# Output gates of heads 0 to 6 computed ahead of the mixers, six of them by seven products, and the scans moved under the next head's q and k

## The chip, the cores and the metric

One core of a Trainium2 chip runs the whole block. The metric is device microseconds from start to end of the program. The kernel before takes 1549.74 us (median of three runs, 1549.45 to 1550.22).

## What is computed

The block takes 1024 frames of 1024 features, sets 16 learned meta tokens ahead of them (T = 1040 tokens), and mixes tokens by eight heads of two kinds: four mLSTM heads with input and forget gates, four retention heads with rotary positions. The parts that matter here, in the reference's terms:

```python
u = rmsnorm(x, mix_g)
# per head: q, k (128 wide), v (256 wide), output gate o (256 wide), all u @ w_in
h = mlstm_chunkwise(conv_silu(q), conv_silu(k), v, li, lf)     # heads 0 to 3
h = retention_chunkwise(rotary(q), rotary(k), v, log_gamma)    # heads 4 to 7
mixed = head_norm(h, g) * (sigmoid(o) if mLSTM else silu(o))
x = x + mixed @ w_out
x = x + gated_conv_mlp(rmsnorm(x, ffn_g))
```

The output gate o of a head needs nothing but u and its weights; it is used only where the scan's normalized output is mixed.

## The kernel before

Every product in float32 accuracy is made of three TensorE passes: both operands are split into a high and a low part (hi on ACT, lo = x - hi on DVE), and hi*hi, hi*lo, lo*hi are summed in PSUM. u is held as such pairs, uh and ul, eight blocks of 128 features by 1040 tokens.

**The mixers.** A first phase makes v of head 0 chunk by chunk as the input lands, with the first norm beside it (`first_norm`, `rms`: row sums by TensorE, square root on ACT, reciprocal on DVE, broadcast back by TensorE into tiles named pra). Then come q and k of head 0, with `gates` (the mLSTM gates: scans along rows on DVE, two rows stored to DRAM as `scr`) and `tables` (which reads them back into the tables A1 and A2, broadcast to all partitions). Then each head h goes through three stages:

- o: `o_group`, six groups (two halves of 128 gate columns by three pieces of 386, 384 and 256 tokens). Under them run the head's first scans: `scan_a` (scores, masks, splits) and `scan_b` (numerator, state), chunks 0 to 3.
- v of head h+1: `v_group`, nine chunks. Under them the rest of the scans and `post_steps` of head h: head norm, transposes (tiles tr), the mixing with the gate (tile mx), and its store to DRAM (`mxd`).
- q and k of head h+1: `qk_group`, six groups with convolution or rotation on DVE. Nothing runs under these.

`merge` deals the side work out among the main groups in code order; a list scheduler then sets each engine's own order, so that all that is said on positions below is read from the finished order.

**Weights.** `units` is a list of weight blocks in the order of their use; `need` asks for one and issues some blocks ahead. A raw block (512 KB) goes into one of two slots (`raw_tile`), its hi and lo parts into one of three. A raw slot is free again when hi and lo have been made of it. Two blocks of w_out per head ("m" units, `last_two`) are used otherwise: they stay in their slot until DVE has multiplied them with the mixed values of the last two tokens (tile mm) and added them to acc, twice 128x1024. In the list they stand after the o blocks of the next head, ahead of v: o(h), o(h), m(h-1), m(h-1), v(h+1), v(h+1), q(h+1), k(h+1).

**Behind the mixers** come w_out, up and gate, and down, each by seven block products in place of eight (Strassen's scheme): sums of weight blocks and of activation blocks are made once, and tiles of 256 and 258 columns are multiplied. The weight sums are made by DMA (`wsum`), dealt out over the mixers' stages.

Of the kernel before, what the change touches and what calls it, by code (L numbers as in the profile page):

```python
# [31 lines left out]
XW = SEQ // 2 + 2  # L32
EPS = 1e-6
# [28 lines left out]
def body(ctx, tc, h_in, vecs, cst, mask_in, rot, w_v0, w_v, w_fm, w_out, w_up, w_gate, w_down, out):  # L62
# [3 lines left out]
    per = ctx.enter_context(tc.tile_pool(name="per", bufs=1))  # L66
    wraw = ctx.enter_context(tc.tile_pool(name="wraw", bufs=2))
# [14 lines left out]
    resid = per.tile([P, KB, T], F32, name="resid")  # L82
# [3 lines left out]
    accseg = ExitStack()  # L86
    accp = accseg.enter_context(tc.tile_pool(name="accp", bufs=1, side="right"))

    acc = accp.tile([P, 2, D], F32, name="acc")
    mm = accp.tile([P, 2 * 8, 2], F32, name="mm")  # L90
    rring = []
    mixed = ExitStack()
    mxp = mixed.enter_context(tc.tile_pool(name="mxp", bufs=1, side="right"))
    mxd = [dram.tile([P, SEQ], F32, name=f"mxd{i}") for i in range(16)]
    epsc = per.tile([P, 1], F32, name="epsc")
    Rb = per.tile([P, T], F32, name="Rb")

# [13 lines left out]


# [20 lines left out]
    def issue(upto):  # L133
        while issued[0] < min(upto, len(units)):
# [8 lines left out]
            sub = 2 if key[:2] == ("v", 0) else 1  # L143
# [61 lines left out]

    u_v(0)
# [108 lines left out]
    mix = ExitStack()  # L315
    st = mix.enter_context(tc.tile_pool(name="st", bufs=1))
    wk = mix.enter_context(tc.tile_pool(name="wk", bufs=2))

    cols = st.tile([P, 3, R36], F32, name="cols")
    dec = st.tile([P, R36], F32, name="dec")  # L320
    sigs = [st.tile([P, 2, PIECES[1][1] - KEEP], F32, name="sig"), mxp.tile([P, 2, T - PIECES[2][0]], F32, name="sig2")]

    def sig(b, p):
        t0, t1, _ = PIECES[p]
        return sigs[1][:, b] if p == 2 else sigs[0][:, b, max(t0, KEEP) - KEEP:t1 - KEEP]
    gts = st.tile([P, 2, NCH, H], F32, name="gts")
    nc.gpsimd.memset(gts[:, :, 0, :], 0.0)
    scr = dram.tile([2, R36, P], F32, name="scr")

    Rc = st.tile([P, NCH], F32, name="Rc")  # L330
    Rg = st.tile([P, H, NCH], F32, name="Rg")
    ug = st.tile([P, KB, 32], F32, name="ug")
    mask = st.tile([P, P], F32, name="mask")
# [56 lines left out]
    def qk_group(h, kind, p):  # L390
# [7 lines left out]
        if h < H:  # L398
# [13 lines left out]
            if h == 0 and kind == "q" and p == 0:  # L412
                after(x, last["sqrt"])
# [102 lines left out]
    def tables(h):  # L516
        if h > H:
            return
# [476 lines left out]
    for h in range(8):  # L995
# [4 lines left out]
        if h == 7:  # L1000
            break
# [6 lines left out]

# [576 lines left out]
```

## Time and profile before

| | |
|---|---|
| median of three runs | 1549.74 us |
| the profiled execution | 1551.16 us, span 1549.4 us |
| granted TensorE clock, mean | 0.992 |
| start of q of head 0, end of the first phase | 37.6 us |
| start of the o gates of head 0 | 64.0 us |
| o gates, v, q and k of one head, heads 4 and 5 | 28.22, 31.23, 23.96 us |
| start of w_out | 701.7 us |

A row of a profile names the source line, the engine, the operation, what is written and read, the count, and after the bar the busy time and the mean of one in ns, then the idle time of the engine ahead of it and what ended it. In rows of windows, each engine's busy time in that stretch follows its length; then come the granted clock, the DMA share and GB/s.

### The profile page before, as it was taken

The numbers are of one execution on the slowest core, as the hardware profiler recorded it, in microseconds if no ns is written. First come the engines' busy times: TensorE is split into PE (matmuls) and PEld (weight loads), VectorE is DVE, ScalarE is ACT, GpSimd is POOL, SyncE is SP. The second block draws the span as 40 slices with busy tenths as digits, with TensorE's granted clock in tenths as the row PEclk, the third lists the DMA queues.
The fourth block names the chain that finished last, engine by engine and source line by source line (L and its number), as shares of the span: only waits on it lengthen the run. The fifth ranks groups of instructions, "written<-read, shape, count | busy, mean of one in ns | idle before, by whom it ended". The sixth has DMA issues, their size and how long they took to land.

```text
span 1549.4 us, 25346 instructions
## 1 busy us (share of the span) xinstructions
PE 1520.5 (98%) x9763; PEld 1398.9 (90%) x9763; DVE 1085.4 (70%) x2312; ACT 735.2 (47%) x1491; POOL 90.5 (6%) x107
## 2 busy tenths in 40 slices
PE   8989999999999999999999999999999999999997
PEld 8989999999999999997788998999999999888887
DVE  8756758686866565678867778766666666778657
ACT  7565555554242433435454455444444444434443
POOL 0110112112120210000000000000000000000000
PEclk9999999999999999999999999999999999999998
DMA  5676768778777773226542225332222224933213
GB/s 190 153 165 165 137 160 193 167 189 181 192 167 179 148 160 90 64 74 245 189 138 97 87 95 185 102 102 83 82 82 82 76 82 142 378 103 111 95 41 109
DMA packets 104904, 212.35 MB, mean 137 GB/s; under 512 B 9352, under 2 KB 31568, under 8 KB 104784
## 3 DMA queue, kind: packets, MB, share of 16 engines
q1 hardware_dynamic: 86096, 175.80, 33.9%
q0 software_dynamic: 18544, 34.87, 14.9%
q8 instruction: 76, 1.25, 0.3%
q14 instruction: 44, 0.36, 0.1%
q10 hardware_dynamic: 144, 0.07, 0.0%
HBM read 181.31 MB, written 84.19 MB: 171 GB/s over the span
## 4 chain that ended last, share of the span: by engine, by line
PE 93%; DMA 3%; DVE 2%; ACT 1%; SPq 0%; issue 0%; DVEq 0%; ACTq 0%
PE pv L374 4%; PE po L386 4%; PE po L384 4%; PE po L385 4%; PE pv L375 4%; PE pv L376 4%; PE pdx L554 3%; PE pdx L556 3%; PE pdx L555 3%; PE pup_x L555 2%; PE pup_x L556 2%; PE pga_x L554 2%; PE pga_x L556 2%; PE pga_x L555 2%; PE pup_x L554 2%; PE pk L384 2%
## 5 line engine op out<-in xcount | busy, mean ns | idle before, releaser
L374 PE MATMUL pv<-hi_v,uh 128*128 128x256 f32 (+1 forms) x512 | 148.4, 290 | 7.6 <-DVE sig L428 3.6
L375 PE MATMUL pv<-lo_v,uh 128*128 128x256 f32 (+1 forms) x512 | 147.6, 289 | 0.0
L376 PE MATMUL pv<-hi_v,ul 128*128 128x256 f32 (+1 forms) x512 | 145.8, 286 | 0.0
L384 PE MATMUL po<-uh,hi_o 128*128 128x386 f32 (+2 forms) x384 | 124.7, 325 | 0.0
L386 PE MATMUL po<-uh,lo_o 128*128 128x386 f32 (+2 forms) x384 | 122.6, 319 | 0.0
L385 PE MATMUL po<-ul,hi_o 128*128 128x386 f32 (+2 forms) x384 | 122.5, 319 | 0.0
L374 PEld LDWEIGHTS pv<-hi_v,uh 128*128 128x128 f32 x512 | 98.2, 192 | 11.6 <-DVE sig L428 3.8
L375 PEld LDWEIGHTS pv<-lo_v,uh 128*128 128x128 f32 x512 | 98.1, 192 | 0.8 <-DVE lo_v L150 0.8
L376 PEld LDWEIGHTS pv<-hi_v,ul 128*128 128x128 f32 x512 | 97.9, 192 | 0.0
L243 ACT CAST hi_up<-raw_up 128x512 fp32r<-128x512 f32 (+1 forms) x52 | 36.4, 719 | 106.7 <-PE pga_z L555 61.2
L384 PEld LDWEIGHTS po<-uh,hi_o 128*128 128x128 f32 x384 | 72.4, 188 | 0.2
L385 PEld LDWEIGHTS po<-ul,hi_o 128*128 128x128 f32 x384 | 72.4, 188 | 0.1
L386 PEld LDWEIGHTS po<-uh,lo_o 128*128 128x128 f32 x384 | 72.3, 188 | 0.0
L244 DVE TENSOR_TENSOR lo_ga<-fraw_ga,hi_ga 128x512 fp32r<-128x512 f32 (+1 forms) x52 | 41.8, 807 | 37.8 <-ACT hi_ga L243 37.6
L554 PE MATMUL pup_x<-uh_g,hi_up 128*128 128x256 f32 (+1 forms) x240 | 67.2, 282 | 0.4 <-ACT uh_g L1024 0.4
L555 PE MATMUL pup_x<-ul_g,hi_up 128*128 128x256 f32 (+1 forms) x240 | 67.4, 283 | 0.1
L244 DVE TENSOR_TENSOR lo_up<-raw_up,hi_up 128x512 fp32r<-128x512 f32 (+1 forms) x52 | 41.3, 808 | 36.0 <-ACT hi_up L243 35.2
L556 PE MATMUL pup_x<-uh_g,lo_up 128*128 128x256 f32 (+1 forms) x240 | 66.3, 282 | 0.0
L194 POOL DMA_DIRECT2D wsd<-w_down_d x55 | 50.9, 1026 | 262.8 <-DMA wsd<-w_down_d 166.1
L384 PE MATMUL pq<-uh,hi_q 128*128 128x400 f32 (+2 forms) x192 | 62.2, 324 | 3.7 <-DVE vl L350 2.5
L385 PE MATMUL pq<-ul,hi_q 128*128 128x400 f32 (+2 forms) x192 | 62.4, 325 | 0.0
L386 PE MATMUL pk<-uh,lo_k 128*128 128x400 f32 (+2 forms) x192 | 62.1, 324 | 0.0
(751 smaller groups left out, 5009.9 us busy)
## 6 DMA issues: line engine op xcount, KB each, us to landing
wsd<-w_down_d SPq DMA_DIRECT2D x22, 512.0 KB, 6.6
wsd<-w_down_d POOLq DMA_DIRECT2D x22, 512.0 KB, 6.5
raw_up<-w_up_d SPq DMA_DIRECT2D x22, 512.0 KB, 3.9
fraw_ga<-w_gate_d SPq DMA_DIRECT2D x22, 512.0 KB, 3.9
acts<-cv SPq DMA_DIRECT2D x44, 256.0 KB, 2.0
rd<-wsd SPq DMA_DIRECT2D x22, 512.0 KB, 3.3
wsd<-w_down_d POOLq DMA_DIRECT2D x33, 256.0 KB, 5.1
raw_o<-w_fm_d SPq DMA_DIRECT2D x16, 512.0 KB, 3.8
```

The source lines that it names most:

```text
L194: nc.gpsimd.dma_start(x, v, accum_op=ALU.add)
L243: nc.scalar.copy(hi[:, o:o + n], x)
L244: nc.vector.tensor_tensor(lo[:, o:o + n], x, hi[:, o:o + n].bitcast(F32), ALU.subtract)
L374: nc.tensor.matmul(pv[:L, :nv], a, hi[:, o:o + nv], start=kb == 0, stop=False)
L375: nc.tensor.matmul(pv[:L, :nv], a, lo[:, o:o + nv], start=False, stop=False)
L376: nc.tensor.matmul(pv[:L, :nv], b, hi[:, o:o + nv], start=False, stop=kb == KB - 1)
L384: nc.tensor.matmul(pt[:, :n], a, uh[kb][:, t0:t1], start=kb == 0, stop=False)
L385: nc.tensor.matmul(pt[:, :n], a, ul[kb][:, t0:t1], start=False, stop=False)
L386: nc.tensor.matmul(pt[:, :n], b, uh[kb][:, t0:t1], start=False, stop=kb == KB - 1)
L554: m.append(nc.tensor.matmul(pt, ah, xh_, start=first and k == 0, stop=False, skip_group_check=True))
L555: nc.tensor.matmul(pt, ah, xl_, start=False, stop=False, skip_group_check=True)
L556: m.append(nc.tensor.matmul(pt, al, xh_, start=False, stop=last and k == n - 1, skip_group_check=True))
```

## The change

- Gates of head 0 are made in the first phase, as the input lands (`o_first`), in place of v of head 0; their product with the norm goes to DRAM (`sgd`) by way of two tiles.
- `ocomb` then builds four combinations of the halves of u (tokens and features each in two halves) from the residual tile, in place, and splits them in hi and lo.
- `o_seven` makes the gates of heads 1 to 6, by seven products each over blocks of 256 and 258 columns, and stores them to `sgd`. `ostep` makes the weight sums on DVE. `sgload` reads a head's gates back when it is mixed.
- v of head 0 is now a stage of its own, with nothing under it; then q and k of head 0.
- Head h below 7: the first scans run under q and k of head h+1, the rest and `post_steps` under v of head h+1. The o stage is gone, except for head 7, which keeps the old form. Tables A and the q and k tiles are there twice, in the place of the residual, which is read again from the input at head 7.
- The mixed values are written over the gate tile (`sig`), no longer into mx.
- The list of weights is: o0, o1 to o6 (four steps each), v0, q0, k0, then q(h+1), k(h+1), m(h-1), m(h-1), v(h+1), v(h+1).

```diff
+    u_f(0, "o")
+    ou = [(h, s) for h in range(1, 7) for s in range(4)]
+    ou.insert(ou.index((1, 1)), ou.pop(ou.index((2, 0))))
+    for h, s in ou:
+        units.append((("o", h, s), lambda h=h, s=s: ostep(h, s)))
     u_v(0)
     u_f(0, "q")
     u_f(0, "k")
-    for h in range(8):
-        u_f(h, "o")
+    for h in range(7):
+        u_f(h + 1, "q")
+        u_f(h + 1, "k")
         if h:
             u_m(h - 1)
-        if h < 7:
-            u_v(h + 1)
-            u_f(h + 1, "q")
-            u_f(h + 1, "k")
+        u_v(h + 1)
+    u_f(7, "o")
+    u_m(6)
...
+    def ocomb():
...
+        for k in range(4):
+            nc.scalar.activation(B4[k], B4[k], AF.Copy, scale=g4[k])
+            nc.vector.scalar_tensor_tensor(B4[k], B1[k], g1[k], B4[k], ALU.mult, ALU.subtract)
+            nc.vector.tensor_tensor(B1[k], B1[k], A1_[k], ALU.subtract)
+            nc.vector.scalar_tensor_tensor(A1_[k], A1_[k], g1[k], B4[k], ALU.mult, ALU.subtract)
...
+            put(4, k, A1_[k])
+        for k in range(4):
+            put(3, k, B1[k], g1[k])
+        for k in range(4):
+            put(5, k, B4[k])
+        for k in range(4):
+            nc.vector.scalar_tensor_tensor(A4[k], A4[k], g4[k], A1_[k], ALU.mult, ALU.subtract)
+            put(6, k, A4[k])
...
+    def o_seven(h):
...
+        for n, (bank, s, o, x) in enumerate(PROD):
+            hi, lo = need(("o", h, s), 2)
+            xs = oblk(x)
+            for ci, (j0, j1) in enumerate(OC):
...
+                m = mm3s(pt, [tuple(v[:, o * HB + k * P:o * HB + (k + 1) * P] for v in (hi, lo)) for k in range(4)],
+                         [tuple(v[:, j0:j1] for v in xs[k]) for k in range(4)], n in (0, 1, 3), n in (1, 5, 6))
...
-        merge([lambda b=b, p=p: (o_group(h, b, p), p == 1 and wsum_next()) for b in range(2) for p in range(3)],
-              [A(0)] + [B(c) for c in range(4 if h < 7 else NCH)])
         if h == 7:
+            resid = rp.tile([P, KB, T], F32, name="resid2", tag="R")
+            for kb in range(0, KB, 2):
+                nc.sync.dma_start(resid[:, kb:kb + 2], h_in[:, kb:kb + 2])
+        for p in range(3):
+            sgload(h, p)
+        if h == 7:
+            merge([lambda b=b, p=p: o_group(h, b, p) for b in range(2) for p in range(3)], [A(0)] + [B(c) for c in range(NCH)])
             break
+        tables(h + 1)
+        merge([lambda kind=kind, p=p: (qk_group(h + 1, kind, p), (kind, p) == ("k", 0) and wsum_next()) for kind in "qk" for p in range(3)], [A(0)] + [B(c) for c in range(4)])
         side = post_steps(h, 0) + [B(4), B(5), B(6)] + post_steps(h, 1) + [B(7), B(8)] + post_steps(h, 2)
         merge([lambda c=c: (v_group(h + 1, c)(), c == 4 and wsum_next()) for c in range(NCH)], side)
-        tables(h + 1)
-        for kind in "qk":
-            for p in range(3):
-                qk_group(h + 1, kind, p)
```

**How the instructions move.** First DVE, around the second accumulation of head 4's last tokens (acc from raw_m9). Before, it stands among the evacuations of k of head 5 (rk5, kT), ahead of the lo part of v of head 6 and of all evacuations of head 5's gates (sig from po5):

```order
L179 SCALAR_TENSOR_TENSOR acc_89<-raw_m9_6436,mm_90,acc_89 128x1024 x2
L418 TENSOR_TENSOR kT_187<-kT_187,rk5_1_6258 128x384
L415 TENSOR_TENSOR rk5_2_6288<-pk5_2_6263,A2_185 64x256
L416 TENSOR_TENSOR rk5_2_6288<-pk5_2_6263,A2_185 64x256
L417 TENSOR_TENSOR kT_187<-pk5_2_6263,A1_184 128x256
L150 TENSOR_TENSOR lo_v_6_0_6645<-raw_v_6_0_6642,hi_v_6_0_6644 128x1024
L418 TENSOR_TENSOR kT_187<-kT_187,rk5_2_6288 128x256
L428 TENSOR_TENSOR sig_175<-po5_0_0_6297,Rb_111 128x386
L428 TENSOR_TENSOR sig_175<-po5_0_1_6324,Rb_111 128x384
```

Now, on the same engine, the same accumulation, which stands behind the evacuation of the last k group of head 6 (pk6_2, ten rows ahead of these), with the lo part of the second half of v of head 6 eight rows behind it:

```order
L930 TENSOR_TENSOR pt5_4l_7491<-pt5_4_7479,pt5_4h_7490 128x128
L959 SCALAR_TENSOR_TENSOR pt5_5_7627<-s5_5_7625,cs_76 128x128
L1013 BN_AGGR mv5_0_7280<-bn5_1_7376 128x2
L197 SCALAR_TENSOR_TENSOR acc_2102<-raw_m9_7300,mm_2103,acc_2102 128x1024 x2
L1008 SCALAR_TENSOR_TENSOR C5_3_7506<-C5_2_7438,u5_3_7494 128x256
L930 TENSOR_TENSOR qd5_4l_7487<-qT_2113,qd5_4h_7486 128x128
L1012 BN_STATS bn5_2_7444<-num5_0_7279 128x6
L930 TENSOR_TENSOR S5_2l_7441<-C5_2_7438,S5_2h_7440 128x256
L959 SCALAR_TENSOR_TENSOR pt5_6_7694<-s5_6_7692,cs_76 128x128
L962 TENSOR_TENSOR kwl5_5_7630<-s5_5_7625,kwh5_5_7629 128x128
L930 TENSOR_TENSOR pt5_5l_7639<-pt5_5_7627,pt5_5h_7638 128x128
L168 TENSOR_TENSOR lo_v_6_1_7524<-raw_v_6_1_7521,hi_v_6_1_7523 128x1024
```

So between acc and the use of the slot by v there stood a stage of gates, and there is none now.

Second PE, at the start of v of head 6, where the second halves of the products wait (hi_v_6_1; the first halves of two groups, pv6_1 and pv6_2, stand ahead of it):

```order
L420 MATMUL pv6_2_7598<-hi_v_6_0_7517,uh1_85 128x256
L421 MATMUL pv6_2_7598<-lo_v_6_0_7518,uh1_85 128x256
L422 MATMUL pv6_2_7598<-hi_v_6_0_7517,ul1_86 128x256
L409 MATMUL pv6_0_7533<-raw_v_6_1_7521,ug_97 32x256 x4
L969 MATMUL u5_4_7644<-vh_2119,kwh5_4_7481 128x256
L970 MATMUL u5_4_7644<-vl_2120,kwh5_4_7481 128x256
L971 MATMUL u5_4_7644<-vh_2119,kwl5_4_7482 128x256
L420 MATMUL pv6_1_7557<-hi_v_6_1_7523,uh2_87 128x256
```

Before, each group of v ran through all eight blocks at once; now two of them are cut in halves, with scans between.

Third PE at the start of the seven products, head 1, where the broadcasts of the first norm (pra400 from column 400 on, pca784 from 784 on) stand among the products:

```order
L698 MATMUL po1_y0_706<-uh3_89,hi_o1_0_655 128x256
L363 MATMUL pra400_548<-cs_76,Rc_95 128x128 x3
L699 MATMUL po1_y0_706<-ul3_90,hi_o1_0_655 128x256
L700 MATMUL po1_y0_706<-uh3_89,lo_o1_0_656 128x256
L698 MATMUL po1_y0_706<-uh3_89,hi_o1_0_655 128x256
L699 MATMUL po1_y0_706<-ul3_90,hi_o1_0_655 128x256
L700 MATMUL po1_y0_706<-uh3_89,lo_o1_0_656 128x256
L351 MATMUL pca784_568<-cs_76,ssa784_555 128x1 x2
```

Before, they stood among the products of q of head 0:

```order
L384 MATMUL pq0_1_734<-uh3_84,hi_q_0_0_237 128x384
L308 MATMUL pra400_580<-cs_73,Rc_180 128x128 x3
L385 MATMUL pq0_1_734<-ul3_85,hi_q_0_0_237 128x384
L386 MATMUL pq0_1_734<-uh3_84,lo_q_0_0_238 128x384
L296 MATMUL pca784_607<-cs_73,ssa784_594 128x1 x2
```

The DVE work that these broadcasts need now stands among the operations of `ocomb`; one piece of it:

```order
L509 SCALAR_TENSOR_TENSOR resid_79<-resid_79,vec_75 128x514
L1110 TENSOR_TENSOR sqh_210<-sqh_210 128x512
L504 SCALAR_TENSOR_TENSOR x3l_590<-resid_79,vec_75,x3h_589 128x514
L509 SCALAR_TENSOR_TENSOR resid_79<-resid_79,vec_75 128x514
L504 SCALAR_TENSOR_TENSOR x3l_590<-resid_79,vec_75,x3h_589 128x514
L517 SCALAR_TENSOR_TENSOR resid_79<-resid_79,vec_75 128x514
L1111 TENSOR_TENSOR ssa784_555<-sqh_210 128x256
```

The sum of squares from column 784 on (ssa784), which the last broadcast needs, now follows updates of the residual tile and low parts of a combination (x3l).

More of the change, by code (lines that the diff above doesn't have):

```diff
@@ L32 @@
 XW = SEQ // 2 + 2
+OS = KEEP - 2
+OW = (T - OS) // 2
 EPS = 1e-6
@@ L984, in body @@
     first_norm(3)
+    for b in range(2):
+        nc.scalar.activation(so[b], so[b], AF.Sigmoid)
+        nc.sync.dma_start(sgd[b], so[b])
+    ocomb()
     for h in range(H):
```

251 lines of the change are left out of this document (186 added, 65 removed).

## The prediction

> **What bounds the kernel now.** I read the page first: busy shares, then the chain that ended last.
>
> ```profile
> PE 1520.5 (98%) x9763; PEld 1398.9 (90%) x9763; DVE 1085.4 (70%) x2312; ACT 735.2 (47%) x1491; POOL 90.5 (6%) x107
> PE 93%; DMA 3%; DVE 2%; ACT 1%; SPq 0%; issue 0%; DVEq 0%; ACTq 0%
> ```
>
> TensorE is busy all the time and is 93% of the chain, so work taken from it shortens the kernel, and each stall put into it lengthens it. VectorE (DVE) stands at 70%, which is an average; so I cut the span at the first matmuls of the stages (starts read from the timeline). In these windows the columns are the length, then busy time by engine, the granted clock, the DMA share and GB/s. They are, in order: o gates of head 0 with its first scans; v of head 1 with the later scans; o gates of head 1; v of head 2; q and k of head 2; then o gates of head 4, v of head 5, q and k of head 5.
>
> ```profile
> 64.00:91.30 27.30, 26.43 (x171) 24.98 (x170) 11.13 (x38) 14.63 (x21) 5.47 (x6) 1.00 0.61 110
> 91.30:136.50 45.20, 38.88 (x292) 37.06 (x292) 28.05 (x88) 28.86 (x74) 4.65 (x5) 0.89 0.62 142
> 161.58:189.47 27.89, 27.89 (x189) 27.22 (x187) 18.72 (x48) 14.56 (x29) 6.38 (x8) 1.00 0.78 142
> 189.47:221.86 32.39, 32.39 (x273) 30.92 (x273) 19.23 (x64) 16.58 (x44) 4.62 (x5) 1.00 0.69 164
> 221.86:249.33 27.47, 24.95 (x161) 24.31 (x159) 20.71 (x55) 15.38 (x30) 2.12 (x2) 1.00 0.73 203
> 418.87:447.09 28.22, 28.22 (x195) 27.98 (x193) 18.45 (x49) 10.32 (x28) 7.11 (x8) 1.00 0.79 146
> 447.09:478.32 31.23, 31.23 (x270) 30.32 (x270) 18.36 (x55) 17.31 (x42) 4.65 (x5) 1.00 0.70 163
> 478.32:502.28 23.96, 23.96 (x157) 23.92 (x155) 19.58 (x39) 4.63 (x9) 2.11 (x2) 1.00 0.83 230
> ```
>
> The reader is to see three things. PE fills the steady stages. DVE is evenly spread: 18 to 20 us in each stage of 24 to 32. And v of head 1 took 45.20 us where v of head 2 took 32.39. What was waited for there, and in the 27.47 us stage, stands in the waits of PE; the granted clock after two of the waits in the windows behind them.
>
> ```profile
> PE pv L374 <- DVE sig L428: 3.6, 1, 3.6
> PE pq L384 <- DVE vl L350: 2.5, 1, 2.5
> 97.75:104.58 6.83, 5.53 (x24) 5.24 (x25) 4.19 (x14) 6.80 (x19) 1.07 (x1) 0.50 0.69 220
> 131.90:135.30 3.40, 3.40 (x17) 3.40 (x18) 2.12 (x8) 2.84 (x9) 0.00 (x0) 0.50 0.20 59
> ```
>
> **Part 1, seven products.** The price of a matmul is the distance of two starts, not the mean duration (starts overlap). Two stretches of the timeline, a gate group and a seven-product stage of the FFN:
>
> ```profile
> 420.13 0.34 PE L385 MATMUL po<-ul,hi_o 128*128 128x386 f32 x1
> 422.41 0.34 PE L386 MATMUL po<-uh,lo_o 128*128 128x386 f32 x1
> ...
> 1006.93 0.28 PE L555 MATMUL pup_x<-ul_g,hi_up 128*128 128x258 f32 x1
> 1007.78 0.29 PE L556 MATMUL pup_x<-uh_g,lo_up 128*128 128x258 f32 x1
> 1008.01 0.28 PE L554 MATMUL pup_y<-xh,hi_up 128*128 128x256 f32 x1
> 1008.96 0.28 PE L556 MATMUL pup_y<-xh,lo_up 128*128 128x256 f32 x1
> ```
>
> Thirteen steps of 386 columns take 2.28 us, 0.175 each or 0.455 ns per column; seven of 258 take 0.85, 0.121 each; eight of 256 take 0.95, 0.119 each. A head's gates are 48 rounds (8 blocks, 3 products, 2 weight blocks) over 386 + 384 + 256 = 1026 columns: 48 x 1026 x 0.455 ns = 22.4 us. By seven products they are 7 x 4 x 3 = 84 pairs of 0.119 and 0.121: 20.2 us. Six heads: **-13 us**. Head 0 keeps its cost, in the first phase, in place of v of head 0, which gets a stage of its own.
>
> **Part 2, stalls that go.** The gate vectors of head 0 run through the DRAM rows scr into the tables A of the first scan; now the six heads' products lie ahead of all that, so v of head 1 no longer shows 45.20 - 32.39 = 12.8 us, nor q of head 2 its 2.5: **-15.3**. But the chain itself stays. The scores of the gates are now ready only with v of head 0, and only q and k of head 0 and a part of q and k of head 1 lie over it. I put back **+3** (0 to 12.8).
>
> **Part 3, the start.** The first products stand right behind the first phase, and DVE must first make the four combinations (32 operations of 514 columns) besides the rest of the first norm, the splits of weights and the evacuations. Nearest rows:
>
> ```profile
> 18.00:29.40 11.40, 11.40 (x94) 11.07 (x93) 11.30 (x30) 11.37 (x27) 0.00 (x0) 1.00 0.21 82
> 29.40:37.60 8.20, 7.20 (x61) 7.01 (x59) 6.15 (x13) 4.73 (x14) 0.00 (x0) 1.00 0.22 66
> L1266 DVE SCALAR_TENSOR_TENSOR cv<-s0up,vec,cv 128x512 f32<-128x512 f32 x20 | 15.0, 751 | 0.4
> L1249 DVE TENSOR_TENSOR s3ga<-pga_x,s3ga 128x512 f32<-128x512 f32 x10 | 6.9, 691 | 1.4 <-PE pga_x L556 0.8
> ```
>
> DVE is full up to 29.4 us; the first phase ends at 37.6, and I take that for the new one too, since it has nearly as many matmul columns on the same input. From there stand 32 x 0.7 = 23 us of combinations and some 15 us of the rest ahead of the operand of the third product: about 60 to 68 us. PE reaches that place after the first phase and some 110 products of 0.12: 51. PE also meets the broadcasts of the first norm (pra, pca) on the way, which wait for reciprocals that the DVE order has put among the combinations. **+13** (5, if ACT and DVE split this better, to 22). From head 2 on, DVE has in each head some 20 operations of this size, 12 to 14 us in 20, and is no limit. Handing the memory over to the mixer's tiles behind the last store: +1.
>
> **Part 4, the start of v of heads 2 to 7: the largest term.** Raw weights have two slots. Before, the two blocks of w_out (raw_m) followed the o weights and had the k stage and o gates to be used up in; the second half of v was split about six gate groups ahead of its use. Now the units run q, k, m, m, v, v, and the slot of the second v half comes free with the second accumulation (acc). That needs the last two columns of the head before, whose last transposes now stand inside the last k group; on DVE acc stands behind that group's evacuation. Its price by rows:
>
> ```profile
> L179 DVE SCALAR_TENSOR_TENSOR acc<-raw_m,mm,acc 128x1024 f32<-128x1024 f32 x26 | 32.2, 1278 | 1.7 <-DMA raw_m<-w_out_d 1.7
> L816 DVE TENSOR_TENSOR kwl<-s,kwh 128x128 fp32r<-128x128 f32 x32 | 9.1, 285 | 3.2 <-ACT kwh L815 3.2
> L146 SPq DMA_DIRECT2D raw_v<-w_v_d x18: 327/330/504, 1.8 to 586.5; - x18
> DMA to landing us min/median/max: 3.4/4.3/8.2
> L149 ACT CAST hi_v<-raw_v 128x1024 fp32r<-128x1024 f32 x14 | 14.7, 1049 | 47.4 <-DMA raw_v<-w_v_d 30.0 <-PE pk L385 11.7 <-PE po L385 5.7
> L150 DVE TENSOR_TENSOR lo_v<-raw_v,hi_v 128x1024 fp32r<-128x1024 f32 x14 | 17.1, 1220 | 5.9 <-ACT hi_v L149 5.8
> ```
>
> For head 6, counted from the evacuation of the last k group: twelve small operations (0.17 to 0.5, as the 0.285 here) with lo_v of the first half (1.22), 4.6 us; acc twice 1.28, 2.6; issue 0.3; landing 4.3; hi 1.05; lo 1.22: 14.1 us. PE has, from the end of that group, some 66 matmuls of 0.12 (scans and the first halves of two v groups), 7.9 us, less 1.2 for the evacuation itself: 6.7. **It stalls 7.4 us**: 6.5 with the shortest landing, 11.3 with the longest. The other heads differ in how far down acc stands (4 to 8.5 us instead of 7.2); over the six I take 6.5, **+39**. For a second reason DVE can't be early: the scans now lie under q and k, so DVE has 18.45 + 19.58 - 3 (gate evacuations) = 35 us there, and PE only 23.96 + 28.22 - 22.4 = 29.8.
>
> After a wait of 3.6 us the trace shows 6.83 us at clock 0.50, another time 3.40 us; after one of 2.5 us none. Half the clock costs half of it, 1.7 to 3.4 us; six times 1.7: **+10** (0 to 20). The Trainium skill, page "TensorE: Matmul & The Clock Gate", Part 1, says the array drops to half clock after a window of about 3.4 us of idleness and needs about one such window of work to come back, which speaks against a change that puts six waits of this size in. Here one stretch was one window long and another two; by the page the term is 10, by the longer row 20.
>
> **Sum.** -13 - 15.3 + 3 + 13 + 1 + 39 + 10 = +37.7 on the profiled execution's 1551.16 us: 1588.9. That execution is 1.4 us above the median of the runs shown (1549.74), so **1587.5**. The later phases (w_out, FFN, down) I take as unchanged. With all ends low (gate chain 0, start 5, stall 4, no half clock) it is +1.7, 1553; with all high (12.8, 22, 11.3, 20) +95, 1646; both at once are less likely than the middle.
>
> **The rivals.**
> - *Faster: the slot is no wait.* If v's second half lands while PE still has covered work (k groups held up by their own evacuations, so that scans pile up behind them and cover the load), the stall is about 1 us and brings no half clock; with the start at 6: -13 - 15.3 + 0 + 6 + 1 + 6 = -15.3, or **1534**. The deciding point is a mean stall of about 3 us with a short start. For it: in the trace raw_v was waited for 30.0 us by ACT and PE took no harm. Against: there six gate groups lay between. Chance 0.27.
> - *Slower by DVE.* If DVE sets the length of the q and k stage (35 against 29.8), T comes 5 us later each time: six stalls of 11 and half clocks of 2.5: **1620**. For it: the 35 us; against: while PE stalls, DVE catches up. Chance 0.13.
> - *About the same.* Only the start is as costly as its high end (20), v stalls of 1.5 us, no half clock: -13 - 15.3 + 3 + 20 + 1 + 9 = +4.7, **1554**. Chance 0.08.
> - The forecast: 0.52.
>
> **How the numbers follow.** About 3 us (0.2%) is what a measurement can tell. Faster is the first rival, with a little of the third: 0.28. Same: 0.05, from the third. Slower: the forecast, the second and the rest of the third, 0.67. The likeliest case's own range is 1560 to 1605; the range reaches down to the first rival and up towards the second: 1532 to 1612.
>
> **What would show it.** In the waits of PE: pv waiting for hi_v or lo_v (or for raw_v) about six times for 4 to 10 us, with granted clock 0.50 behind it; raw_v's issue right behind acc. At the start: waits of po for DVE between 38 and 70 us. Six heads of gates in about 120 us show part 1. The forecast is wrong if v of heads 2 to 7 starts without a wait of over 3 us, or if these stages, with q and k, take less than 62 us per head.

## The result, and the profile after

The changed kernel takes 1625.77 us (median of four runs, 1622.42 to 1627.84) against 1549.98 for the kernel before in the same comparison: 1.0482 times as long (95% interval 1.0456 to 1.0507), 76 us more. The forecast had the sign, and half the size: 1587.5, range to 1612.

The page of the changed kernel, busy shares and chain:

```profile
PE 1547.6 (95%) x9955; PEld 1413.1 (87%) x9955; DVE 1139.9 (70%) x2429; ACT 740.4 (46%) x1533; POOL 89.9 (6%) x102
PE 84%; DVE 6%; DMA 5%; ACT 2%; issue 1%; SPq 0%; DVEq 0%; ACTq 0%
```

PE's share of the chain fell from 93% to 84%; DVE, DMA and ACT have come into it. Where, the windows show, cut at the stages again. They are: the start of the seven products; the rest of them; v of head 0; q and k of head 1; v of head 1; q and k of head 2; v of head 2; q and k, then v, of head 5; the o gates of head 7; the remainder.

```profile
40.20:78.00 37.80, 29.69 (x223) 28.33 (x223) 35.19 (x72) 20.60 (x41) 1.20 (x1) 0.91 0.38 104
78.00:175.30 97.30, 97.30 (x817) 97.17 (x819) 57.36 (x101) 42.25 (x79) 15.03 (x16) 1.00 0.95 224
175.30:206.60 31.30, 26.29 (x210) 25.49 (x210) 8.84 (x30) 6.70 (x12) 7.14 (x8) 0.89 0.91 193
230.20:272.40 42.20, 30.08 (x180) 28.38 (x178) 23.62 (x69) 24.93 (x51) 5.45 (x6) 0.84 0.59 104
272.40:311.80 39.40, 36.23 (x290) 34.43 (x290) 25.48 (x81) 20.28 (x54) 5.09 (x5) 0.96 0.69 176
311.80:347.80 36.00, 31.08 (x210) 29.85 (x208) 30.45 (x93) 18.05 (x42) 4.14 (x5) 0.96 0.59 129
347.80:382.70 34.90, 34.44 (x265) 32.33 (x266) 22.37 (x73) 18.75 (x45) 6.78 (x7) 0.90 0.93 223
525.30:554.40 29.10, 28.82 (x198) 28.23 (x196) 22.48 (x60) 6.29 (x22) 5.82 (x7) 1.00 0.70 146
554.40:590.00 35.60, 33.65 (x278) 31.43 (x279) 23.87 (x68) 17.02 (x47) 3.15 (x3) 1.00 0.73 184
725.10:780.80 55.70, 47.18 (x270) 42.74 (x268) 37.67 (x110) 30.20 (x75) 0.00 (x0) 0.82 0.66 247
780.80:1622.40 841.60, 831.00 (x4792) 728.70 (x4791) 599.09 (x986) 382.48 (x694) 1.40 (x2) 0.99 0.35 117
```

The products themselves run as forecast: 97.3 us without a gap (811 of the six heads' 1008 products). Nearly every stage around them is longer than without stalls. The first w_out matmul starts at 780.8 us, 79.1 later than before (701.7); behind it 6.1 us come back (841.6 against 847.7), since head 7's scans used to run on under w_out and are now done before it. Where the time lies, stage by stage (the time without stalls is the forecast's own; each stage is read from one profiled execution):

| stage | measured, us | without stalls | more |
|---|---|---|---|
| up to v of head 0 | 175.3 | 37.6 + 6 x 20.2 = 158.8 | 16.5 |
| v of head 0 | 31.3 | 24.5 | 6.8 |
| q and k of head 1 | 42.2 | 29.8 | 12.4 |
| v of head 1 | 39.4 | 31.2 to 32.4 | 7 to 8 |
| q, k and v of heads 2 to 4, each | 70.9, 71.8, 70.8 | 61 to 62.3 | 27.9 |
| q, k and v of heads 5 to 7, each | 64.8, 67.5, 67.6 | 61 | 16.9 |
| o gates of head 7 | 55.7 | 32.7 | 23.0 |

The last column adds up to 111. Without stalls (q and k of head 0, 23.6 us, had none) w_out would have started at 670, 32 us ahead of the 701.7 of before; 111 less 32 are the 79. The 45 us of heads 2 to 7 can be split further: in their 413.3 us PE stood idle for 23.6 and ran 37.4 us at half clock, which is 18.7 us if PE alone had set the pace there.

```profile
311.80:725.10 413.30, 389.72 (x2831) 370.39 (x2830) 300.12 (x852) 172.00 (x443) 50.43 (x55) 0.95 0.66 155
```

The waits of PE, the forecast's place among them:

```profile
PE n L969 <- ACT num L1000: 12.5, 20, 2.5
PE u L971 <- DVE kwl L953: 10.6, 1, 10.6
PE po_x L698 <- DVE soh L483: 5.1, 2, 4.3
PE pv L420 <- DVE gts L398: 5.0, 1, 5.0
PE pv L409 <- DMA raw_v<-w_v_d: 4.2, 6, 2.1
PE pv L421 <- DVE lo_v L168: 2.0, 1, 2.0
```

For the weights of v PE waits 7.5 us in all (raw_v and lo_v as here, and 1.3 for hi_v), where the forecast wanted 39; the longest of these waits took 2.1 us. The longest sum stands at n, the numerator of the scan, which waits for its copy (num) on ACT. What ACT's copy waits for stands in ACT's waits of the mixers, before and after:

```profile
ACT num L857 <- PE tr L901: 17.8, 9, 6.1
```

```profile
ACT num L1000 <- PE tr L1044: 76.8, 18, 7.7
ACT num L1000 <- DVE num L988: 11.6, 3, 9.7
```

ACT's copy waited 76.8 us, 18 times, for the transposes: those of an earlier piece (tr) must empty the one tile num before the next piece may be written into it. From here on this is theory N; the forecast's raw weight slot is theory S.

### The profile page after: what moved, and what is told of

The parts are those of the page before. It is cut to its first block, busy times and chain, and to the rows that moved or that the text cites. A ratio compares the mean times of both kernels' runs of the same rounds, so it can differ in the third digit from the quotient of the medians.

```text
span 1622.4 us, 26048 instructions
## 1 busy us (share of the span) xinstructions
PE 1547.6 (95%) x9955; PEld 1413.1 (87%) x9955; DVE 1139.9 (70%) x2429; ACT 740.4 (46%) x1533; POOL 89.9 (6%) x102
## 3 DMA queue, kind: packets, MB, share of 16 engines
q0 software_dynamic: 18544, 34.87, 14.2%
## 4 chain that ended last, share of the span: by engine, by line
PE 84%; DVE 6%; DMA 5%; ACT 2%; issue 1%; SPq 0%; DVEq 0%; ACTq 0%
PE pv L420 4%; PE pv L421 4%; PE pv L422 4%; PE pdx L698 3%; PE pdx L700 3%; PE pdx L699 3%; DMA Rt<-scr 2%; PE pup_x L699 2%; PE pup_x L700 2%; PE pup_x L698 2%; PE pga_x L698 2%; PE pga_x L699 2%; PE pga_x L700 2%; PE pwx L699 2%; PE pdy L698 2%; PE pdy L700 2%
## 5 line engine op out<-in xcount | busy, mean ns | idle before, releaser
L422 PE MATMUL pv<-hi_v,ul 128*128 128x256 f32 (+1 forms) x512 | 149.6, 293 | 0.0
L421 PEld LDWEIGHTS pv<-lo_v,uh 128*128 128x128 f32 x512 | 102.6, 200 | 2.4 <-DVE lo_v L168 2.2
L422 PEld LDWEIGHTS pv<-hi_v,ul 128*128 128x128 f32 x512 | 102.6, 200 | 0.1
L299 DVE TENSOR_TENSOR lo_ga<-fraw_ga,hi_ga 128x512 fp32r<-128x512 f32 (+1 forms) x52 | 41.9, 810 | 37.4 <-ACT hi_ga L298 37.2
L1000 ACT COPY num<-n 128x257 f32<-128x257 f32 (+3 forms) x72 | 26.6, 370 | 90.3 <-PE tr L1044 76.8
L699 PE MATMUL pup_x<-ul_g,hi_up 128*128 128x256 f32 (+1 forms) x240 | 67.6, 283 | 0.1
L431 PE MATMUL pk<-ul,hi_k 128*128 128x400 f32 (+2 forms) x192 | 62.9, 328 | 0.0
L430 PE MATMUL pk<-uh,hi_k 128*128 128x400 f32 (+2 forms) x192 | 62.7, 327 | 0.0
L432 PE MATMUL pq<-uh,lo_q 128*128 128x400 f32 (+2 forms) x192 | 62.4, 325 | 0.0
L431 PE MATMUL pq<-ul,hi_q 128*128 128x400 f32 (+2 forms) x192 | 62.1, 323 | 0.0
L299 DVE TENSOR_TENSOR lo_d<-rd,hi_d 128x1024 fp32r<-128x1024 f32 (+1 forms) x34 | 37.7, 1115 | 34.0 <-ACT hi_d L298 34.0
L700 PE MATMUL pdx<-uh_d,lo_d 128*128 128x512 f32 (+1 forms) x156 | 58.3, 377 | 0.0
```

The source lines that it names most:

```text
L299: nc.vector.tensor_tensor(lo[:, o:o + n], x, hi[:, o:o + n].bitcast(F32), ALU.subtract)
L421: nc.tensor.matmul(pv[:L, :nv], a, lo[:, o:o + nv], start=False, stop=False)
L422: nc.tensor.matmul(pv[:L, :nv], b, hi[:, o:o + nv], start=False, stop=kb == KB - 1)
L430: nc.tensor.matmul(pt[:, :n], a, uh[kb][:, t0:t1], start=kb == 0, stop=False)
L431: nc.tensor.matmul(pt[:, :n], a, ul[kb][:, t0:t1], start=False, stop=False)
L432: nc.tensor.matmul(pt[:, :n], b, uh[kb][:, t0:t1], start=False, stop=kb == KB - 1)
```

## The experiments

Unless a row says otherwise, the numbers are medians of four runs and the ratio is to the kernel before on the same chip.

**1. A numerator tile for each piece (e1_num).** Heads 0 to 6 shared num0 although num1 and num2 lie there for head 7:

```diff
-            base = mxp.tile([P, 4, DV + 2], F32, tag=f"num{p if h == 7 else 0}", name=f"num{h}_{p}", bufs=1)
+            base = mxp.tile([P, 4, DV + 2], F32, tag=f"num{p}", name=f"num{h}_{p}", bufs=1)
```

Expected: 

> The changed kernel, with a numerator tile of its own for each of the three pieces of a head (num0, num1, num2 for all heads; before only head 7 had them, and all pieces of heads 0 to 6 shared one). Theory S (the raw weight slot held by the w_out block, as in the prediction): the tile is no part of it, 1620 to 1630 us. Theory N (the scans of a head can't go on until the transposes of the piece before have emptied the one numerator tile, and with the scans under q, k and v the chain of scans has no slack left): most of the 44 us that the pairs of stages of heads 2 to 7 take above 61 to 62 each, and most of the 23 us more in the o stage of head 7, go: 1560 to 1580 us, the o stage of head 7 at 33 to 36 us.

Measured: 1574.8 us, ratio 1.0135 (1.0099 to 1.0171): 51 us of the 76 are gone. The waits of ACT's copy for tr are no longer in the list; its wait is now for the matmul itself. The q and k stage and the v stage of head 3, and the o gates of head 7, in this kernel:

```profile
381.30:408.10 26.80, 26.80 (x182) 26.50 (x181) 22.05 (x55) 8.64 (x20) 4.44 (x5) 1.00 0.84 195
408.10:443.40 35.30, 34.11 (x286) 32.37 (x286) 28.78 (x98) 20.38 (x57) 4.88 (x5) 1.00 0.69 167
694.90:727.10 32.20, 31.57 (x223) 31.21 (x222) 23.69 (x68) 16.13 (x42) 0.00 (x0) 1.00 0.55 187
```

Head 3 takes 62.1 us in place of 71.8, at full clock; head 7's gates 32.2 in place of 55.7. Theory N holds for the heads from 3 on and for the 23 us that the forecast did not have. The six pairs of stages fell from 413.3 us to 385.6, so 28 of their 45 us went with the tile; head 2's pair did not fall (72.0 against 70.9; see 14 and 15). Idle time and half clock went together here (PE's idle time from 23.6 to 9.8 us, half clock from 37.4 to 3.4), so what each was worth is not told apart.

**2. The w_out blocks behind v (e2_mlate), 3. both (e3_both).**

```diff
-        if h:
-            u_m(h - 1)
         u_v(h + 1)
+        if h:
+            u_m(h - 1)
```

Expected: 

> The changed kernel, with the two w_out blocks of head h-1 listed behind v of head h+1 in place of ahead of it, so that no slot that v needs hangs on an accumulation. Theory S: most of the 39 us of stalls and the half clocks behind them go: 1580 to 1590 us. Theory N: within 5 us of the changed kernel, 1620 to 1630.

Expected: 

> Both edits, numerator tiles and late w_out blocks. Theory S: as the late blocks alone, 1580 to 1590. Theory N: as the numerator tiles alone, 1560 to 1580, and at most 5 us below it. If both waits are real and one hides behind the other: over 10 us below the better of the two.

Measured: 1633.42 us (1.0511, 1.0471 to 1.0552) and 1582.11 us (1.0186, 1.0157 to 1.0215). PE's waits for the weights of v are gone in both traces, so the edit does what it is for; yet by the ratios the kernels are 4 and 8 us slower than without it (the intervals of each pair overlap, but both are on the same side, where theory S wanted a gain of tens). Theory S falls.

**4. No combinations (e4_nocomb).** The call of ocomb is left out, and the products read x1, x0, x2, x0 where they read x3 to x6, so that the gates of heads 1 to 6 are not computed:

```diff
+        x = {3: 1, 4: 0, 5: 2, 6: 0}.get(x, x)
...
-    ocomb()
```

Expected: 

> The changed kernel without the four combinations of u: ocomb isn't called, and the products that read them read plain blocks of u (so the gates of heads 1 to 6 are other numbers); all matmuls stay. If the combinations on DVE make the stall at the start of the seven products (8 us of idle PE and 6.8 us at half clock between 40 and 78 us), 10 to 16 us go: 1610 to 1616, and v of head 0 starts at about 160 in place of 175. If the first norm or the weights make it, under 5 us: 1621 to 1626.

Measured (one run): 1613.89 us, 12 less; v of head 0 starts at 166.7 in place of 175.3, so 8.6 of the 16.5 us of the start hang on the combinations. Whether PE waits for their results or for other work of DVE that they delay, this run can't tell.

**5. No weight sums in the seven-product phase (e5_nowsum).** On e1_num, the sums move from behind each head's products into the mixers:

```diff
-        wsum_next()
...
-... (kind, p) == ("k", 0) and wsum_next()) ...
+... ((kind, p) == ("k", 0) or (kind, p, h > 1) == ("q", 1, True)) and wsum_next()) ...
```

Expected: 

> The kernel with the numerator tiles (e1_num, 1574.8 us) without weight sums by DMA in the seven-product phase: its six calls go to the q groups of heads 3 to 7. In e1_num the k stage of head 1 waits 13 us for an operand that hangs on the tables read from scr, landing after about 15 us where before had 6.6. Theory C (the weight sums, late in their queue, collide with these loads): landings of 7 to 9 us, that stage at 33 to 37 us in place of 45, 1562 to 1567 us. Theory G (the chain of the gates is simply too long for the work that now lies over it): within 4 us of e1_num, 1571 to 1579.

Measured: 1590.22 us (1.0229, 1.0197 to 1.0261), 15 us slower than e1_num. Theory C is right about the loads: the two large ones of head 1 landed in 10.3 and 11.8 us in place of 17.3 and 17.6, and q and k of head 1 together took 39.3 us in place of 45.1. But the sums cost more under the mixers than under the products: v of heads 2 and 3 took 42.7 and 40.9 us in place of 36.7 and 35.3, and PE waited 12.0 us for raw_v where it had waited 1.1.

**6. Head 1 by plain products (e6_plain1, on e1_num), 7. both (e7_all, on e5_nowsum).** Head 1's gates are made by plain products like head 0's, ahead of the seven products of heads 2 to 6:

```diff
-    for h in range(1, 7):
-        u = sevens[h] if h == 2 else o_seven(h)
...
-        run(u)
+    o_plain(1)
+    for h in range(2, 7):
+        run(o_seven(h))
```

Expected: 

> The kernel with the numerator tiles (e1_num), with the gates of head 1 by plain products (192 matmuls of 256 and 258 columns in place of 168, so 2.9 us more of work) in the place of its seven, so that nothing needs the combinations for some 23 us. If DVE's combinations make the stall at the start: 8 to 11 us less, 1564 to 1567. If the first norm makes it: no gain, 1574 to 1579.

Expected: 

> Numerator tiles, head 1 plain and no weight sums in the seven-product phase together. If both theories (C, and the combinations) hold, the gains add up: 1551 to 1558 us, about the kernel before. If only the combinations do: 1563 to 1568.

Measured: 1573.84 us (1.0116, 1.0074 to 1.0158), no gain that stands out of its interval, though q and k of head 1 took 39.4 us here too, with five of the six sums left where they were; and 1594.06 (1.0252, 1.0208 to 1.0296), as e5 without it. This was no test of the operand: DVE's order still had the combinations ahead of head 1's evacuations. Row 40 to 60 us of e6_plain1, DVE busy all the time:

```profile
40.20:60.00 19.80, 15.50 (x112) 15.41 (x111) 19.80 (x36) 8.26 (x16) 0.00 (x0) 0.83 0.09 27
```

**8. Idle matmuls in head 7's scans (e8_fill)**, on the changed kernel:

```diff
             mm3(up[:, :nv], kw, v, True, True)
+            if h == 7 and not one_bank:
+                for _ in range(6):
+                    nc.tensor.matmul(up[:, 256:512], vh[:, c, :P], vh[:, c, :DV], start=True, stop=True, skip_group_check=True)
```

Expected: 

> The changed kernel with six idle matmuls of 256 columns (into unused columns of the state update's bank) behind each state update of head 7, chunks 0 to 6, 42 in all or 5 us of work; nothing else differs. The o stage of head 7 took 55.7 us with 19.6 us at half clock. If the half clock comes from PE being too little used while the scans stand alone, and costs what it takes (10 us): half-clock time there falls below 10 us and the stage to 47 to 53 us. If the chain between the engines alone sets that tail, the clock costing nothing: 55 to 60 us.

Measured (two runs): 1623.3 us, 2.5 less than the changed kernel, inside the spread of its runs. The o stage of head 7 shows 34.8 us at full clock:

```profile
732.90:767.70 34.80, 32.33 (x227) 31.70 (x225) 20.18 (x52) 16.00 (x36) 0.00 (x0) 1.00 0.56 207
```

but the scans' end only slid under w_out: the last numerator matmul stands at 796 us in place of 781, and the FFN's first pup_x at 998.8 in place of 994.6. So the stage by itself proves nothing, and this run does not tell what half clock costs. Its trace shows two other things. The time at half clock within the first 1000 us is 75 us in place of 102, but half of that difference lies ahead of 725 us, where both kernels have the same instructions in the same order; there the run with less half clock was 8 us later (v of head 1 took 44.2 us in place of 39.4). That is how far two executions can differ, and stage times of single profiles are to be read so. And the first phase, the changed kernel first, then this one:

```profile
0.00:40.20 40.20, 36.53 (x214) 34.47 (x215) 32.84 (x78) 31.69 (x76) 0.31 (x5) 0.87 0.56 191
0.00:41.00 41.00, 37.71 (x215) 35.59 (x216) 33.57 (x79) 32.31 (x76) 0.31 (x5) 1.00 0.55 187
```

With 10.2 us at half clock it took no longer than with none. So time at half clock can cost nothing, and isn't to be booked as loss by itself.

**9. Tables loaded later (e9_tab), 10. staging tiles moved (e10_of).** Both on e1_num. In e9 the tables of the next head are called for behind the last k group; in e10 the tiles `of` get a pool on the other side:

```diff
-        tables(h + 1)
+        if h + 1 >= H:
+            tables(h + 1)
...
+... (kind, p) == ("k", 2) and h + 1 < H and tables(h + 1)) ...
```

```diff
+    ofp = first.enter_context(tc.tile_pool(name="ofp", bufs=1, side="right"))
...
-            return cp.tile([P, OW], F32, tag="of", name=f"of{n}_{h}", bufs=5)
+            return ofp.tile([P, OW], F32, tag="of", name=f"of{n}_{h}", bufs=5)
```

Expected: 

> The kernel with the numerator tiles (e1_num, 1574.8 us), with the tables of head h+1 loaded from scr behind the last k group of head h+1 in place of ahead of its q groups (heads 1 to 3). In the changed kernel the loads for heads 0 and 1 are issued together, at 241.5 to 245.4 us, 1 MB each, and land in 15 us where before one head's landed alone in 6.6. Theory T (they share the DMA): landings of 6 to 9 us, the k stage of head 1 at 22 to 27 us in place of 32, 1564 to 1570 us in all. Theory G (the gate chain is too long by itself): 1571 to 1579.

Expected: 

> e1_num with the staging tiles of the seven products (of) at the other end of the memory, under acc, so that the v tiles of the mixers don't lie where the last gate stores are read from. v of head 0 took 31.3 us, and its first evacuation waited for the clearing of vh, which waited for the store of head 6's gates (landing 8.3 us). If that hand-over is the cause: v of head 0 at 24.5 to 27 us, and 4 to 7 us less in all, 1568 to 1571. If the gates' or the norm's data are: within 3 us of 1574.8.

Measured: e9 1577.34 us (1.0166, 1.0127 to 1.0205): nothing, because the scheduler issued the loads where they had been. e10 1575.12 us (1.0144, 1.0122 to 1.0166): v of head 0 as expected, 25.2 in place of 31.3, but the sum is that of e1_num; v of head 2 took 43.0 us in place of 36.7. First the one, then the other:

```profile
174.90:200.10 25.20, 24.55 (x209) 23.73 (x209) 8.60 (x30) 6.73 (x12) 5.50 (x6) 1.00 0.90 212
338.90:381.90 43.00, 38.12 (x283) 35.72 (x282) 32.05 (x97) 25.80 (x63) 6.80 (x7) 0.88 0.77 186
```

**11. Low parts on GpSimd (e11_pool), 12. the sum (e12_sum).** e11 is e1_num with the low parts of the unscaled combinations on GpSimd; e12 has the edits of 9, 10 and 11 in one:

```diff
-                nc.vector.tensor_tensor(lo, src, hi.bitcast(F32), ALU.subtract)
+                nc.gpsimd.tensor_tensor(lo, src, hi.bitcast(F32), ALU.subtract)
```

Expected: 

> e1_num with twelve of the sixteen low parts of the combinations on GpSimd in place of DVE (128x514; the nearest row, 128x256 on GpSimd, took 0.72 us where DVE takes 0.42). If the sheer load of DVE between 40 and 60 us (19.8 busy of 19.8) is what the start waits for: 12 x 0.6 = 7 us are taken from it, 3 to 7 us less, 1568 to 1572. If GpSimd's slower pace or its share of the memory port gives it back: 1574 to 1582.

Expected: 

> Numerator tiles, late tables, the staging tiles moved and the low parts on GpSimd together. If the three last gains are separate they add up: 1552 to 1562 us. If they sit on one chain (gates late either way), no more than the best of them alone: 1564 to 1570. Below 1546 it would beat the kernel before.

Measured: 1588.57 us (1.0225, 1.0203 to 1.0247) and 1580.47 (1.0177, 1.0152 to 1.0203): e11 is 11 us slower than e9 and 13 than e10 on the same chip, e12 no gain over either. GpSimd needs two to four times DVE's 0.67 us for a low part. DVE itself became slower beside it: in e11, five of its operations of 512 or 514 columns took 1.02 to 1.78 us, all five while GpSimd was at a low part, where the others and those of e1_num took 0.62 to 0.74. Two rows of GpSimd and two of DVE:

```profile
L501 POOL TENSOR_TENSOR x4l<-resid,x4h 128x514 fp32r<-128x514 f32 x4 | 10.5, 2631 | 43.1 <-ACT x4h L500 43.1
L501 POOL TENSOR_TENSOR x6l<-resid,x6h 128x514 fp32r<-128x514 f32 x4 | 5.1, 1316 | 12.5 <-DMA sgd<-sol 12.5
49.36 1.78 DVE L504 SCALAR_TENSOR_TENSOR x3l<-resid,vec,x3h 128x514 fp32r<-128x514 f32 x1
51.73 0.74 DVE L504 SCALAR_TENSOR_TENSOR x3l<-resid,vec,x3h 128x514 fp32r<-128x514 f32 x1
```

**13. Head 1's tables held back for real (e13_hold)**, on e10:

```diff
+        def late(kind, p):
+            if h == 0 and (kind, p) == ("k", 1):
+                for x in A12(1):
+                    nc.vector.tensor_copy(x[:, 0:1], QK(1)[1][:, 783:784])
+                    nc.vector.tensor_copy(x[:, META:META + 1], QK(1)[1][:, 783:784])
+                tables(1)
```

Expected: 

> e10_of (1575.1 us, 1.0144 of the kernel before on the same chip), with the tables of head 1 held back for real: four one-column copies from k of head 1 (its second piece) go into the tables ahead of the loads, so that these wait for that piece; the late-tables run had not moved them, its loads still stood behind those of head 0. Theory T (the two heads' loads share the DMA): the tables of head 0 land in 6 to 9 us in place of 15, the k stage of head 1 takes 22 to 27 us in place of 32.3, ratio 1.007 to 1.011. Theory G (the gate chain by itself is too long): k stage 29 to 33 us, ratio 1.012 to 1.017.

Measured: 1569.56 us, ratio 1.0104 (1.0089 to 1.0119), 0.004 below e10. The k stage of head 1 in e10 and in this kernel:

```profile
236.70:269.00 32.30, 17.18 (x97) 15.95 (x95) 16.53 (x49) 15.05 (x38) 3.54 (x4) 0.79 0.55 107
```

```profile
236.80:261.10 24.30, 17.07 (x101) 16.16 (x99) 16.36 (x51) 13.08 (x32) 3.82 (x4) 0.86 0.52 102
```

8 us gone, the time that theory T had forecast, but not by its mechanism. The rows of DVE, e10 first, show the mask added to the first table of head 0 (the first row of each), the first use of its second table (qd), and the kwl that PE waits for (12.4 us in e10):

```profile
243.12 1.23 DVE L678 TENSOR_TENSOR Rt<-Rt,mask 128x1024 f32<-128x1024 f32 x1 [2.58 <-DMA Rt<-scr]
247.21 0.29 DVE L957 TENSOR_TENSOR qd<-Rt 128x128 f32<-128x128 f32 x1 [2.25 <-DMA Rt<-scr]
258.97 1.23 DVE L678 TENSOR_TENSOR Rt<-Rt,mask 128x1024 f32<-128x1024 f32 x1 [5.84 <-DMA Rt<-scr]
260.80 0.34 DVE L954 SCALAR_TENSOR_TENSOR kwl<-s,cols,kwh 128x128 fp32r<-128x128 f32 x1
```

```profile
242.58 1.22 DVE L678 TENSOR_TENSOR Rt<-Rt,mask 128x1024 f32<-128x1024 f32 x1 [1.84 <-DMA Rt<-scr]
246.22 0.29 DVE L957 TENSOR_TENSOR qd<-Rt 128x128 f32<-128x128 f32 x1 [1.80 <-DMA Rt<-scr]
251.66 0.35 DVE L954 SCALAR_TENSOR_TENSOR kwl<-s,cols,kwh 128x128 fp32r<-128x128 f32 x1
```

Head 0's tables were there by 247 us in e10 too; the hold brought them 1 us forward. What went is the third row of e10, the mask added to head 1's table, at which DVE stood ahead of the scan of head 0. That addition now waits in v of head 1 (4.95 us, at 280 us), and 4 of the 8 us came back there (38.4 against 34.1).

**14. Head 1 plain, and DVE's order set (e15_plainlast)**, on e13; besides the plain products:

```diff
-            nc.scalar.activation(B4[k], B4[k], AF.Copy, scale=g4[k])
-            nc.vector.scalar_tensor_tensor(B4[k], B1[k], g1[k], B4[k], ALU.mult, ALU.subtract)
+            after(nc.scalar.activation(B4[k], B4[k], AF.Copy, scale=g4[k]), last["sqrt"])
+            after(nc.vector.scalar_tensor_tensor(B4[k], B1[k], g1[k], B4[k], ALU.mult, ALU.subtract), last["rec"])
```

Expected: 

> e13_hold with the gates of head 1 by plain products (2.9 us more of work) and, on DVE, the combinations ordered behind the last reciprocal of the first norm. In the run with head 1 plain alone the combinations still stood ahead of the norm and of head 1's evacuations on DVE, and PE waited as before. If the order on DVE is the cause of the start stall (11 us between 40 and 80 us): 8 to 10 us of it go, 5 to 8 us net of the added work, ratio 0.003 to 0.006 below e13_hold. If DVE's sum of work is (19.8 of 19.8 us busy), less than 2 us.

Measured: 1563.45 us, ratio 1.006 (1.0041 to 1.0078), 0.0044 below e13. Between 40 and 60 us PE now has no gap:

```profile
40.20:60.00 19.80, 19.80 (x171) 19.80 (x170) 14.02 (x30) 13.08 (x22) 0.00 (x0) 1.00 0.12 41
```

Run 6 has the same plain products, and the gap: in this stretch it is the order on DVE that makes it, and not the sum of its work. The order alone, with head 1 by seven products, was not run. v of head 0 starts 2.6 us sooner (172.2 against 174.8), with 2.9 us more of work ahead of it; the rest of the gain lies in later stages, and no run ties it to a cause. v of head 2 was still 43.2 us. Its DVE timeline around the table of head 3 (the mask added, L691):

```profile
357.10 0.61 DVE L1065 SCALAR_TENSOR_TENSOR sig<-tr,vec,sig 128x386 f32<-128x386 f32 x1
364.25 1.23 DVE L691 TENSOR_TENSOR Rt<-Rt,mask 128x1024 f32<-128x1024 f32 x1 [6.54 <-DMA Rt<-scr]
365.39 0.28 DVE L944 TENSOR_TENSOR pt_8l<-pt,pt_8h 128x128 fp32r<-128x128 f32 x1
```

DVE stands 6.54 us at an addition whose load hasn't landed, with the scan's splits queued behind it.

**15. The mask added later (e16_addlate)**, on e15: the addition is a function of its own, called in the v stage and ordered behind chunk 7's evacuation.

```diff
+        x = nc.vector.tensor_tensor(A1[:, :META], A1[:, :META], m[:, :META], ALU.add)
+        if order:
+            after(x, last["vl"])
```

Expected: 

> e15_plainlast (1.006 of the kernel before), with the adding of the mask to the tables of heads 1 to 3 ordered on DVE behind the evacuation of chunk 7 of the v stage before; the loads stay where they are. In that run DVE came to this addition for head 3 before its load had landed and stood 6.5 us at it, with ACT and the scans behind it, and v of head 2 took 43.2 us where 34 would do, v of head 1 38.1. Theory D (DVE, waiting in order at a load, holds the scans up): v of head 1 at 34 to 36 us, v of head 2 at 34 to 37, together 8 to 12 us less, ratio 0.998 to 1.001. If the scans are late for another reason: ratio 1.004 to 1.008. Under 0.998 it would beat the kernel before.

Measured (twelve runs): 1552.21 us, ratio 0.9988 (0.9972 to 1.0004). v of heads 1 and 2:

```profile
256.90:290.80 33.90, 33.90 (x283) 32.07 (x283) 25.88 (x93) 19.57 (x54) 3.15 (x3) 1.00 0.87 214
321.80:354.50 32.70, 32.70 (x275) 31.00 (x275) 26.33 (x89) 23.02 (x56) 3.18 (x3) 1.00 0.84 190
```

33.9 and 32.7 in place of 38.1 and 43.2. So theory D holds, and the whole loss of the change is undone; no version was found that beats the kernel before clear of its interval. w_out starts at 702.9 us here, 33 later than without stalls: 13 of them lie ahead of v of head 0, 9 from there to the end of v of head 1, 11 in the pairs of heads 2 to 7. That is what still eats the gain that the change was made for, and its causes stay open.

**16. The w_out blocks once more (e17_mlate2)**, the edit of 2 on e16.

Expected: 

> e16_addlate (0.9988 of the kernel before, 0.9972 to 1.0004) with the w_out blocks of head h-1 behind v of head h+1 in the list of weights, as in e2_mlate. There the wait for the raw slot could have been hidden behind the scans that stood at the one numerator tile; here that cover is gone. Theory S, what is left of it: 5 to 15 us less, ratio 0.989 to 0.995. If the slot holds nothing up (PE waits 0.8 us for raw_v in the run without it): 0.997 to 1.002, or a little slower, as the same edit was before (by 7 us, twice).

Measured (twelve runs): 1560.8 us, ratio 1.0051 (1.0031 to 1.007): slower again, this time clear of the intervals. PE's 0.8 us of waits for raw_v are gone, so the slot held nothing up here either; why the edit costs time stays open.

## Why the prediction was wrong

- **Part 1, seven products: right.** 97.3 us without a gap for the last 4.8 heads is 20.2 us a head, as reckoned.
- **Part 2, stalls that go: too small by some 23 us.** The +3 put back for the gates' chain was the term of a range to 12.8, from a trace in which one head's tables were loaded alone. Now two heads' tables went out together; q and k of head 1 took 12.4 us more than its work, v of head 1 7 to 8 more, v of head 0 6.8. The first is DVE standing in order at the tables: in the changed kernel at head 0's (5.3, 2.6 and 7.6 us) and at head 1's (1.9), ahead of the kwl that PE waited 10.6 us for; the hold (13) shows it for head 1's. Why head 0's second table took 15.4 us to land was not separated. Of the second, 5 us went with the numerator tile (34.1 us in e1_num); the hold brought 4 back, and the late addition (15) took these away again. The third was a store of the last gates that v's tiles had to wait for (10), which the forecast had at 1 us.
- **Part 3, the start: near, by luck in part.** +13 and 1 against 16.5. The forecast let PE wait for the operand of the third product, at 60 to 68 us; its own figures (37.6 + 23 + 15) give 76 for that. PE hardly waited for a combination there. It waited for DVE to take head 0's gates out of PSUM (soh: 4.3, 1.0 and 0.7 us), which stood behind combinations in DVE's order. The forecast had that order too, for the broadcasts of the norm; (14) shows it to be the cause between 40 and 60 us once head 1 is plain.
- **Part 4, v of heads 2 to 7: the failed step.** The forecast read from the order that the second half of v's weights would come late, and priced a stall of 6.5 us each, +39. The reading of the order was good: for head 6 that half was split 12.6 us behind the last k group, where 14.1 were reckoned, and a load of v stands right behind an accumulation in every head. What failed is the stall that was to follow: PE waited 7.5 us for these weights in all, never longer than 2.1; its longest sum in these stages stood at the numerator's copy (8.6 us), and taking the weights' slot out of the way made three kernels slower (2, 3, 16; clear of the intervals only in the last).
- **What stood in its place.** That pairs of stages came out 45 us longer, near the 39 + 10 forecast, was a coincidence: the single numerator tile made 28 of them (1), and head 2's pair, which the tile left as it was, fell with the late mask addition (63.7 us in 15). The step took a late place in the list for a cause, where it was in part a symptom: with three tiles the second halves were split from 2.1 us ahead of the v stage to 9.3 into it, and not 6.0 to 11.0 into it. The rows of before held a hint that I passed over: ACT's copy already waited 17.8 us for the transposes, while PE waited 0.8 us for that copy. That the q and k stages, without scans, gave it the slack is argued, not run: the kernel before was not tried with three tiles.
- **What the sum lacked:** the o gates of head 7, 23 us, from the same tile. They were taken as unchanged because their code is. (The two extremes of the sum, 1553 and 1646, are counted from 1551.16, the other times from 1549.74.)
- **The second reason in part 4** (DVE with 35 us of work under q and k) was wrong too: the windows show 22 to 30 us there, as the scheduler moved scans on into the v stages, and in e1_num those stages run with PE full in heads 3 to 6.
- **Half clock: more than the forecast had.** In heads 2 to 7 it was 37.4 us, up to 18.7 us of loss against +10 (0 to 20); what it really cost is not shown (8). The forecast tied it to waits of the size of 3.6 us, but its second row, 131.90 to 135.30, stands behind waits of 0.8 and 1.9 us. The Trainium skill, page "TensorE: Matmul & The Clock Gate", Part 1, has the gate answer to how busy PE has been. The trace agrees: half clock came in stages with many waits of PE in a row, none over 2.5 us in heads 2 to 7 and the gates of head 7, and nearly all of it there went when the tile did (1).
- **The rivals.** The first had the slot right (7.5 us over six heads, about its 1 us each), and missed by the tile and the tables. DVE as the bound of q and k is not seen. The third had the v stalls right (1.5 us each), and nothing of the rest.

## What to carry to other kernels

When work that ran in two stages out of three is to run in all of them, look for every single-buffered tile between its steps: a wait that cost nothing had slack in the stage that is now filled. A late position in a scheduled order can be a symptom; what is late there has to be followed to the tile or the load that it waits for, by what ACT and DVE wait for as well as PE. An instruction that waits for a DMA in the middle of an in-order engine holds up all behind it, so it goes where the load has surely landed.

## What the runs showed of the hardware

- Loads of the tables (512 KB each, in rows of 128 numbers to all partitions) landed in 5.3 to 10.8 us in the kernel before, and in 6.5, 15.4, 14.2 and 15.9 us where two heads' were issued within 5 us of each other (the changed kernel). The number of heads is not all of it: in run 13 one head's pair, issued alone at 266 us, took 14.5 and 18.3. In the changed kernel one such issue held its queue for 8.41 us, where others took 0.37.
- GpSimd took 1.3 to 2.6 us for a 128x514 subtraction where DVE takes 0.67, and some of DVE's operations beside it took 1.0 to 1.8 us in place of 0.7 (11).
- Time at half clock can cost nothing: the first phase took 40.2 us with 10.2 us of it at half clock, and 41.0 with none (8).
- Half clock needs no long wait: none of PE's waits in heads 2 to 7 was over 2.4 us, and 37.4 us of their 413.3 ran at half clock.
